# A hybrid encoder layer on one core: low parts and a rotary sum by adding DMAs, gate projections moved to the end of their stage

## The chip, the cores and the metric

The kernel runs on one core of a Trainium2 chip. TensorE (PE) multiplies matrices, VectorE (DVE), ScalarE (ACT) and GpSimd (POOL) work elementwise, and SyncE (SP) issues DMAs; each has a queue of its own that runs in order, and 16 DMA engines move the data. The metric is the device time of one execution in microseconds (us), the median of the runs of one kernel. Lower is better.

## The reference

One layer over 1024 tokens of width 1024, all in float32. Each sub-layer is wrapped in RMS norms, before and after, and its result is added to the residual stream.

```python
h = _rms_norm(x, g_mix_pre[l])
proj = h @ w_in[l]
aq, ak, av, dqkv, dgate, dalpha, dbeta = jnp.split(proj, IN_SPLITS, axis=-1)
aq = _rope(aq.reshape(b, s, ATTN_HEADS, ATTN_HEAD_DIM), positions)
ak = _rope(ak.reshape(b, s, ATTN_KV_HEADS, ATTN_HEAD_DIM), positions)
...
attn_o = _window_attention(aq, ak, av, attn_sink[l]).astype(x.dtype)
dn_o = _gated_deltanet(dqkv, dgate, dalpha, dbeta, ...).astype(x.dtype)
mix = jnp.concatenate([attn_o, dn_o], axis=-1) @ w_out[l]
x = x + _rms_norm(mix, g_mix_post[l])
c = _memory_cross_attention(_rms_norm(x, g_cross_pre[l]), _rms_norm(mem, g_mem[l]), ...)
x = x + _rms_norm(c, g_cross_post[l])
f = _swiglu(_rms_norm(x, g_ffn_pre[l]), w_gate_up[l], w_down[l])
x = x + _rms_norm(f, g_ffn_post[l])
```

The rotary embedding turns each head's two halves against each other: `x1*cos - x2*sin` and `x2*cos + x1*sin`. The attention is windowed (128 tokens to either side, 8 heads of 64, 2 key heads, a sink logit per head). The DeltaNet has 4 heads of 128, runs in both directions, and solves a triangular system in each block before a scan over blocks.

## The kernel before

**Split operands.** TensorE multiplies in a rounded format (fp32r). To keep float32 accuracy, an operand is held as a high part (the rounded value) and a low part (the value minus the high part), and each product is made of three matmuls: high by high, high by low, low by high. `split` (from L99) makes both parts: ScalarE rounds (L102), and VectorE, or GpSimd where the caller asks for it, subtracts (L103). `load_w` loads 512 KB of weights into a tile `wraw` (L125, on SP's queue) and splits it into `whi` and `wlo`. All three have two buffers, so a third load waits until the first raw tile has been read, and a third cast until the matmuls of the first are done. `load_w` runs at a raised priority, ahead of the work around it.

**Stages.** Stage 1 norms and turns the input, projects the DeltaNet's q, k and v (`proj`, matmuls at L261 into PSUM tiles `pg`, three buffers), convolves them on VectorE, and prepares the blocks; `base_inverse` inverts 32x32 blocks in a long chain of small VectorE operations (L534, L536), once for each pair of heads (`B0`, `B1`). Stage 2 has ten more projections, each of two halves of 512 tokens: A0 to A3 are the queries of the attention, A4 its keys, V its values, G0 to G3 the DeltaNet's gates. Beside them run the levels L0 to L3 (one for each DeltaNet head: SP fetches many small blocks of the inverse at L551, PE multiplies at L585 and L591, results are stored at L610), and the windows of the attention (`W` starts two of the 16 and ends the two before). Stage 3 scans the DeltaNet's blocks with the remaining windows and the memory's keys and values beside it. Then come the output projection, cross attention, its output projection, and the feed-forward layer.

**Attention tile.** `attn_proj` takes each half from PSUM, multiplies it by the sine into `sn` (tag "rot", two buffers, L729) and by the cosine into `rop` (two buffers, L730). Four DMAs on SP's queue bring the 32-row groups of `sn` to a tile `rot` in exchanged order (L734), and VectorE adds it (L735). The sum is split, and high and low parts are stored to memory (L739), where a window loads them again as `qs` (L625) or as keys (L679). `value_proj` copies its halves to `vT`, which uses the tag "rot" too (L746). `gate_proj` applies Silu and stores (L758, L759).

**Order.** The lists `ORDER_1` to `ORDER_3` give the program's order. A scheduler turns it into one queue per engine, by priority and by its own model of time, so the engines' queues interleave several items of a list; once built, a queue is fixed and runs in order.

**Mid norms.** `mid_gemm` (matmuls at L1016) makes an output projection for 512 tokens, normalises the result and adds the residual (L1030), then norms the new residual stream for the next sub-layer: ScalarE squares and sums (L1033), GpSimd takes the power (L162), ScalarE scales (L1036). It is called four times with four tiles of 128 tokens. PE then turns the scaled tiles.

**Constants.** `mhalf` and `phalf`, 16 columns each, hold -0.5 and 0.5 for GpSimd's power. They stand in the first pool on the left of the on-chip memory, ahead of the weight tiles.

Of the kernel before, what the change touches and what calls it, by code (L numbers as in the profile page):

```python
# [10 lines left out]
F32 = mybir.dt.float32  # L11
F32R = mybir.dt.float32r
I32 = mybir.dt.int32
AF = mybir.ActivationFunctionType
ALU = mybir.AluOpType
# [4 lines left out]
P = 128  # L20
# [4 lines left out]
HALF = 512  # L25
# [8 lines left out]


ORDER_1 = "D0 P0 D1 P1 D2 B0 P2 D3 P3 B1".split()
ORDER_2 = "L0 L1 G0 G1 A4 V A0 A1 L2 L3 W W W A2 A3 G2 G3 W".split()
ORDER_3 = ("M " + "s01 W K " * 5 + "s01 K " * 3 + "s01 V V").split()


# [35 lines left out]
def tile_hybrid_block(  # L76
# [6 lines left out]
    nc = tc.nc  # L83
    x, mem, out = x[0], mem[0], out[0]
    w_in, w_out, w_cq, w_ckv, w_co = w_in[0], w_out[0], w_cq[0], w_ckv[0], w_co[0]
    w_gate_up, w_down = w_gate_up[0], w_down[0]

    if dump is None:
        def dump(name, ap):
            pass  # L90


    def f32(ap):
        return ap.bitcast(F32)
# [4 lines left out]
    def split(hi, lo, src, scale=None, eng=None):  # L99

        if scale is None:
            nc.scalar.copy(hi, src)  # L102
            (eng or nc.vector).tensor_tensor(lo, src, f32(hi), ALU.subtract)  # L103
        else:
            nc.scalar.activation(hi, src, AF.Identity, scale=scale)
            nc.vector.scalar_tensor_tensor(lo, src, scale, f32(hi), ALU.mult, ALU.subtract)

    def pool(name, bufs, **kw):
        return tc.tile_pool(name=name, bufs=bufs, reuse_waits="tile", **kw)

    cst = ctx.enter_context(pool("cst", 1))
# [6 lines left out]
    def load_w(src, k, n, eng=None, after=None):  # L118

        with tc.high_priority(AHEAD):  # L120
            raw = wp.tile([P, k, n], F32, tag="wraw", name="wraw")
            with ExitStack() as order_:
                if after:
                    order_.enter_context(tc.issue_after(after.ins))
                nc.sync.dma_start(raw, src.rearrange("(k p) n -> p k n", p=P))  # L125
            hi = wp.tile([P, k, n], F32R, tag="whi", name="whi")
            lo = wp.tile([P, k, n], F32R, tag="wlo", name="wlo")
            split(hi, lo, raw, eng=eng)
        return hi, lo
# [2 lines left out]
    ident = cst.tile([P, P], F32, name="ident")  # L132
    mhalf = cst.tile([P, 16], F32, name="mhalf")
    nc.gpsimd.memset(mhalf, -0.5)
    phalf = cst.tile([P, 16], F32, name="phalf")
    nc.gpsimd.memset(phalf, 0.5)
    cols = cst.tile([P, P], F32, name="cols")
    p12 = ExitStack()
# [10 lines left out]
    trp = p1.enter_context(pool("trp", 2, side="right"))  # L149
# [61 lines left out]
    for hf in range(2):  # L211
        hi = hx.tile([P, KT, HALF], F32R, name=f"hhi{hf}")
        lo = hx.tile([P, KT, HALF], F32R, name=f"hlo{hf}")
        for j in range(4):
# [10 lines left out]
            for kq in range(2):  # L225
# [4 lines left out]
                o = slice(4 * kq, 4 * kq + 4), slice(j * P, (j + 1) * P)  # L230
# [25 lines left out]
    def gemm_b(whi, wlo, act, psums, nk=KT):  # L256

        for ah, p_ in zip(act, psums):
            for k in range(nk):
                for i, (w, a) in enumerate(((whi, 0), (whi, 1), (wlo, 0))):  # L260
                    nc.tensor.matmul(p_, w[:, k, :], ah[a][:, k, :], start=(k == 0 and i == 0),  # L261
                                     stop=(k == nk - 1 and i == 2))

    def proj(src_cols, eng=None):
        whi, wlo = load_w(src_cols, KT, P, eng)
        pp = [pg.tile([P, 512], F32, tag="pg", name="pg") for _ in range(2)]
        gemm_b(whi, wlo, hT, pp)
        return pp
# [42 lines left out]
    for hf in range(2):  # L311
        pp = pg.tile([P, 512], F32, tag="pg", name="pg")
# [390 lines left out]
    def issue(order, table):  # L703
        for o in order:
            table[o[0]](*(int(c) for c in o[1:]))
# [13 lines left out]
        nc.gpsimd.memset(t, 0.0)  # L719

    def attn_proj(ct):
        pp = proj(w_in[:, ct * P:(ct + 1) * P])
        dst = [t[ct * P:(ct + 1) * P, :] if ct < 4 else t for t in (d_q if ct < 4 else d_k)]
        for hf in range(2):
            sl = slice(hf * HALF, (hf + 1) * HALF)
            rop = trp.tile([P, HALF], F32, tag="rop", name="rop")
            sn = trp.tile([P, HALF], F32, tag="rot", name="sn")
            rot = trp.tile([P, HALF], F32, tag="rot2", name="rot2")
            nc.vector.tensor_tensor(sn, pp[hf], sinT[:, sl], ALU.mult)  # L729
            nc.vector.tensor_tensor(rop, pp[hf], cosT[:, sl], ALU.mult)  # L730

            for q in range(4):
                o = 32 * (q ^ 1)
                nc.sync.dma_start(rot[32 * q:32 * q + 32], sn[o:o + 32])  # L734
            nc.vector.tensor_tensor(rop, rop, rot, ALU.add)  # L735
            hl = [trp.tile([P, HALF], F32R, tag=t, name=t) for t in ("qhi", "qlo")]
            split(*hl, rop)
            for t, o in zip(hl, dst):
                nc.sync.dma_start(o[:, sl], f32(t))  # L739

    def value_proj():

        pp = proj(w_in[:, 640:768])
        for hf in range(2):
            vT = trp.tile([P, HALF], F32, tag="rot", name="vT")
            nc.scalar.copy(vT, pp[hf])  # L746
            pt = pw.tile([P, 512], F32, tag="pw", name="ptv")
            for j in range(4):
                nc.tensor.transpose(pt[:, j * P:(j + 1) * P], vT[:, j * P:(j + 1) * P], ident)
            pt = pt.rearrange("p (c g e) -> p c g e", c=4, g=2)  # L750
            split(*(vhl[:, 4 * hf:4 * hf + 4, :, i] for i in range(2)), pt)

    def gate_proj(h):

        pp = proj(w_in[:, 2304 + h * P:2304 + (h + 1) * P])
        for hf in range(2):
            gt = trp.tile([P, HALF], F32, tag="rop", name="gt")
            nc.scalar.activation(gt, pp[hf], AF.Silu)  # L758
            nc.sync.dma_start(d_gate[h * P:(h + 1) * P, hf * HALF:(hf + 1) * HALF], gt)  # L759

    issue(ORDER_2, {"A": attn_proj, "V": value_proj, "G": gate_proj, "L": levels, "W": next_windows})
    dump("d_q", d_q); dump("d_k", d_k); dump("d_gate", d_gate)
    p1.close()
# [201 lines left out]
    L0 = ExitStack()  # L965
# [33 lines left out]
    def mid_gemm(tz, act, w, gp, res, dst, hf, between=None):  # L999


        zs = [tz.tile([P, D], F32, tag="z", name="z", bufs=4) for _ in range(4)]
        sss = [tz.tile([P, 2], F32, tag="zss", name="zss", bufs=8) for _ in range(4)]
        for ch in range(2):
            cs = slice(ch * 512, (ch + 1) * 512)
            if ch and between:
                between()
            pp = [pg.tile([P, 512], F32, tag="pg", name="pmg") for _ in range(4)]
            for kp in range(4):
                whi, wlo = load_w(w[kp * 256:(kp + 1) * 256, cs], 2, 512)  # L1010
                for t in range(4):
                    tt = slice(t * P, (t + 1) * P)
                    for kk in range(2):
                        k = 2 * kp + kk
                        for i, (w_, a) in enumerate(((whi, 0), (whi, 1), (wlo, 0))):
                            nc.tensor.matmul(pp[t], act[a][:, k, tt], w_[:, kk, :], start=(k == 0 and i == 0),  # L1016
                                             stop=(k == KT - 1 and i == 2))
            for t in range(4):
                nc.scalar.activation(zs[t][:, cs], pp[t], AF.Square, accum_out=sss[t][:, ch:ch + 1])
                nc.vector.tensor_tensor(zs[t][:, cs], pp[t], gp[:, cs], ALU.mult)  # L1020
        xn = []
        for t in range(4):
            tok = slice(hf * HALF + t * P, hf * HALF + (t + 1) * P)
            z = zs[t]
            xr = tz.tile([P, D], F32, tag="xr", name="xr", bufs=XR)
            nc.sync.dma_start(xr, res[tok, :])
            rs = tz.tile([P, 1], F32, tag="prs", name="prs", bufs=4)
            nc.gpsimd.tensor_scalar(rs, sss[t][:, 1:2], sss[t][:, 0:1], D * EPS, ALU.add, ALU.add)
            nc.gpsimd.tensor_tensor(rs, rs, mhalf[:, 0:1], ALU.pow)
            nc.vector.scalar_tensor_tensor(z, z, rs, xr, ALU.mult, ALU.add)  # L1030
            nc.sync.dma_start(dst[tok, :], z)
            s2 = tz.tile([P, 1], F32, tag="ps2", name="ps2", bufs=4)
            nc.scalar.activation(xr, z, AF.Square, accum_out=s2)  # L1033
            r2 = tz.tile([P, 1], F32, tag="pr2", name="pr2", bufs=4)
            rstd_of(r2, s2, 1.0 / D, EPS)
            nc.scalar.activation(xr, z, AF.Identity, scale=r2)  # L1036
            xn.append(xr)
        return xn

# [4 lines left out]
    L1 = ExitStack()  # L1044
# [28 lines left out]
    L2 = ExitStack()  # L1073
# [63 lines left out]
    L3 = ExitStack()  # L1137
# [326 lines left out]
    for t in range(4):  # L1464
# [14 lines left out]
        xr = residual(r)  # L1479
# [40 lines left out]
```

## Time and profile before

| | |
|---|---|
| median of 3 runs | 1559.16 us (1558.93 to 1559.38) |
| profiled execution, its own time | 1562.86 us |
| its span | 1561.1 us |
| PE busy | 1504.1 us (96%) |
| VectorE busy | 1052.3 us (67%) |
| ScalarE busy | 726.5 us (47%) |
| GpSimd busy | 308.8 us (20%) |
| DMA, mean over the span | 158 GB/s |

In a timeline row stand the start and the length in us, the engine, the line, the operation, what it writes and reads, and in brackets the idle time of the engine before it with what ended that. A row of grouped instructions gives the least, the median and the greatest duration in ns, then the first and the last start in us. In a table by stretches the engines stand in the order PE, PE's weight loads, VectorE, ScalarE, GpSimd, each with its busy time and its number of instructions, then the granted PE clock (1.00 is full), the busy share of the DMA engines and their GB/s. A list of DMAs gives the KB of each and the median us from issue to landing.

### The profile page before, as it was taken

What the parts mean: (1) busy time and instruction counts of PE and PEld (TensorE: products, weight loads), DVE (VectorE), ACT (ScalarE), POOL (GpSimd) and SP (SyncE); (2) the same over time, 40 slices, a digit from 0 to 9 for tenths busy, and PEclk for the clock granted to TensorE, in tenths of its full rate; (3) what the DMA queues carried; (4) which work ended last, traced back from release to release, by engine and by line L of the source; (5) the groups of instructions that cost most, each with busy time, mean ns of one, the idle gap of its engine ahead of it and who ended that gap; (6) DMA issues with size and microseconds to landing.
All of it is one profiled execution on the core that took longest, in us unless ns stands there. A gap on an engine that the chain in (4) does not pass through costs nothing.

```text
span 1561.1 us, 20936 instructions
## 1 busy us (share of the span) xinstructions
PE 1504.1 (96%) x7451; PEld 1252.7 (80%) x7451; DVE 1052.3 (67%) x1742; ACT 726.5 (47%) x1388; POOL 308.8 (20%) x305
## 2 busy tenths in 40 slices
PE   6999999988999999999999999999999999999998
PEld 5888787877899777888888877888888888888786
DVE  6777888767998855434346377776867554696665
ACT  6665552346557765453336574322222222454532
POOL 2000110000004102153102221443433333000021
PEclk9999999999999999999999999999999999999999
DMA  6244446868987674354213254333433334753354
GB/s 208 70 130 121 130 146 159 219 176 273 336 268 251 199 268 149 116 169 147 68 54 135 97 190 139 115 125 119 157 119 109 101 102 138 286 195 102 108 174 164
DMA packets 267367, 247.17 MB, mean 158 GB/s; under 512 B 39016, under 2 KB 204797, under 8 KB 267261
## 3 DMA queue, kind: packets, MB, share of 16 engines
q1 hardware_dynamic: 267261, 245.82, 49.6%
q8 instruction: 59, 0.97, 0.2%
q14 instruction: 47, 0.39, 0.1%
HBM read 173.65 MB, written 69.50 MB: 156 GB/s over the span
## 4 chain that ended last, share of the span: by engine, by line
PE 78%; DVE 7%; DMA 6%; ACT 3%; issue 2%; SPq 2%; POOL 1%; DVEq 0%; POOLq 0%; ACTq 0%
PE pg L261 13%; PE pmg L1016 10%; PE pD L1191 8%; PE pE L1191 8%; PE pA L1191 6%; PE pcq L261 6%; PE pdX L1381 6%; PE pdA L1381 4%; PE pB L1191 4%; PE pdD L1381 2%; PE psc L785 2%; PE pcs L1097 1%; PE pco L1123 1%; DVE wlo L103 1%; PE pdX L1474 1%
## 5 line engine op out<-in xcount | busy, mean ns | idle before, releaser
L102 ACT CAST whi<-wraw 128x1024 fp32r<-128x1024 f32 x108 | 113.1, 1048 | 170.6 <-PE pg L261 38.4
L103 DVE TENSOR_TENSOR wlo<-wraw,whi 128x1024 fp32r<-128x1024 f32 x78 | 95.5, 1225 | 87.4 <-ACT whi L102 83.3
L261 PE MATMUL pg<-hhi,whi 128*128 128x512 f32 x352 | 142.1, 405 | 1.5 <-DVE rop L730 1.5
L261 PE MATMUL pg<-hhi,wlo 128*128 128x512 f32 x352 | 141.0, 401 | 0.0
L261 PE MATMUL pg<-hlo,whi 128*128 128x512 f32 x352 | 141.0, 401 | 0.0
L1016 PE MATMUL pmg<-whi,b 128*128 128x512 f32 x384 | 120.0, 399 | 2.6 <-ACT whi L102 2.2
L1191 PE MATMUL pA<-s,whi 128*128 128x512 f32 x352 | 111.4, 397 | 1.2 <-ACT m L1208 1.2
L103 POOL TENSOR_TENSOR wlo<-wraw,whi 128x1024 fp32r<-128x1024 f32 x30 | 73.9, 2464 | 147.0 <-ACT whi L102 138.8
L1016 PEld LDWEIGHTS pmg<-whi,b 128*128 128x128 f32 x384 | 72.2, 191 | 18.2 <-ACT whi L102 2.6
L261 PEld LDWEIGHTS pg<-hhi,whi 128*128 128x128 f32 x352 | 67.0, 191 | 16.7 <-DVE rop L730 2.0
L261 PEld LDWEIGHTS pg<-hlo,whi 128*128 128x128 f32 x352 | 67.0, 190 | 14.8
L1191 PEld LDWEIGHTS pA<-s,whi 128*128 128x128 f32 x352 | 65.2, 187 | 16.8 <-ACT m L1208 1.9
L261 PEld LDWEIGHTS pg<-hhi,wlo 128*128 128x128 f32 x352 | 66.7, 190 | 14.7
L1381 PE MATMUL pdX<-dhl,whi 128*128 128x512 f32 x264 | 76.1, 390 | 1.5 <-DVE zv L1436 0.8
L1016 PE MATMUL pmg<-wlo,b 128*128 128x512 f32 x192 | 71.5, 392 | 0.0
L1191 PE MATMUL pA<-s,wlo 128*128 128x512 f32 x176 | 69.7, 397 | 1.1 <-DVE wlo L103 1.1
L102 ACT CAST whi<-araw 128x1024 fp32r<-128x1024 f32 (+1 forms) x36 | 35.3, 982 | 71.3 <-PE pdX L1381 27.6
L1268 POOL TENSOR_TENSOR act<-act,up 128x512 f32<-128x512 f32 x33 | 50.1, 1519 | 91.1 <-DVE up L1267 54.3
L103 DVE TENSOR_TENSOR wlo<-araw,whi 128x1024 fp32r<-128x1024 f32 (+1 forms) x36 | 40.8, 1133 | 40.2 <-ACT whi L102 40.2
L286 DVE SCALAR_TENSOR_TENSOR acc<-cp,cols,acc 128x1024 f32<-128x1024 f32 x48 | 61.4, 1281 | 1.5 <-ACT acc L284 0.9
L1381 PEld LDWEIGHTS pdX<-dhl,whi 128*128 128x128 f32 x264 | 49.3, 188 | 12.8 <-issue 1.1
L1241 DVE TENSOR_TENSOR sr<-sr,wraw 128x512 f32<-128x512 f32 x22 | 38.1, 1732 | 29.1 <-POOL sr L1240 29.1
(408 smaller groups left out, 3971.9 us busy)
## 6 DMA issues: line engine op xcount, KB each, us to landing
wraw<-in_w_gate_up_dram SPq DMA_DIRECT2D x52, 512.0 KB, 3.9
kv<-d_kv SPq DMA_DIRECT2D x32, 512.0 KB, 6.7
wraw<-in_w_in_dram SPq DMA_DIRECT2D x22, 512.0 KB, 4.6
b<-in_w_down_dram SPq DMA_DIRECT2D x20, 512.0 KB, 6.8
araw<-d_as SPq DMA_DIRECT2D x20, 512.0 KB, 3.6
pz<-d_pz SPq DMA_DIRECT2D x32, 256.0 KB, 6.5
wraw<-in_w_ckv_dram SPq DMA_DIRECT2D x16, 512.0 KB, 7.1
wraw<-in_w_out_dram SPq DMA_DIRECT2D x16, 512.0 KB, 4.2
```

The source lines that it names most:

```text
L102: nc.scalar.copy(hi, src)
L103: (eng or nc.vector).tensor_tensor(lo, src, f32(hi), ALU.subtract)
L261: nc.tensor.matmul(p_, w[:, k, :], ah[a][:, k, :], start=(k == 0 and i == 0), stop=(k == nk - 1 and i == 2))
L286: nc.vector.scalar_tensor_tensor(acc, cp[:, t:t + S], taps[t], acc, ALU.mult, ALU.add)
L785: nc.tensor.matmul(out[:, d, h, :], lt[:, d, h, :], rt[:, d, h, :], start=True, stop=True)
L1016: nc.tensor.matmul(pp[t], act[a][:, k, tt], w_[:, kk, :], start=(k == 0 and i == 0), stop=(k == KT - 1 and i == 2))
L1097: nc.tensor.matmul(pp[:, t2_, :], q[a][:, ct, tt], kr_[b_][:, ct, :], start=(j == 0 and i == 0), stop=(j == 1 and i == 2))
L1123: nc.tensor.matmul(po, vr_[a][:, kt, cs], pts[kt][b_], start=(kt == 0 and i == 0), stop=(kt == 1 and i == 2))
L1191: nc.tensor.matmul(out_, w[a][:, k, :], xx[b_][:, k, :], start=(start and k == 0 and i == 0), stop=(k == HK - 1 and i == 2), skip_group_ch ...
L1241: nc.vector.tensor_tensor(s[1], s[0], a_[:, 0:HK], ALU.subtract)
L1268: nc.gpsimd.tensor_tensor(o_, o_, up, ALU.mult)
L1381: nc.tensor.matmul(banks[t], a[:, k - k0, tt], w, start=(first and k == 0 and i == 0), stop=(k == NB - 1 and i == 2), skip_group_check=not ...
```

## The change

Five edits:

1. The attention tile's rotary sum: the tile `rot`, the four copies on SP's queue and VectorE's addition go. Four DMAs on GpSimd's queue add the exchanged groups of `sn` into `rop` directly.
2. The low parts of the ten projections' weights: ScalarE writes the negated, rounded value into the low tile, and one DMA on GpSimd's queue, 512 KB, adds the raw weights to it. In `split` the value `nc.sync` for `eng` chooses this way.
3. `ORDER_2`: the two gate projections G0 and G1 move from ahead of A4 to behind A3, and V moves behind A1.
4. In `mid_gemm` VectorE does the last scaling in place of ScalarE.
5. The constant tile `phalf` is allocated with 32 columns, of which 16 are used.

```diff
-ORDER_2 = "L0 L1 G0 G1 A4 V A0 A1 L2 L3 W W W A2 A3 G2 G3 W".split()
+ORDER_2 = "L0 L1 A4 A0 A1 V L2 L3 W W W A2 A3 G0 G1 G2 G3 W".split()
...
         if scale is None:
             nc.scalar.copy(hi, src)
-            (eng or nc.vector).tensor_tensor(lo, src, f32(hi), ALU.subtract)
+            if eng is nc.sync:
+                nc.scalar.mul(lo, src, -1.0)
+                nc.gpsimd.dma_start(f32(lo), src, accum_op=ALU.add)
+            else:
+                (eng or nc.vector).tensor_tensor(lo, src, f32(hi), ALU.subtract)
...
-    phalf = cst.tile([P, 16], F32, name="phalf")
+    phalf = cst.tile([P, 32], F32, name="phalf")[:, 0:16]
...
     def attn_proj(ct):
-        pp = proj(w_in[:, ct * P:(ct + 1) * P])
+        pp = proj(w_in[:, ct * P:(ct + 1) * P], nc.sync)
...
-            rot = trp.tile([P, HALF], F32, tag="rot2", name="rot2")
             nc.vector.tensor_tensor(sn, pp[hf], sinT[:, sl], ALU.mult)
             nc.vector.tensor_tensor(rop, pp[hf], cosT[:, sl], ALU.mult)
 
             for q in range(4):
                 o = 32 * (q ^ 1)
-                nc.sync.dma_start(rot[32 * q:32 * q + 32], sn[o:o + 32])
-            nc.vector.tensor_tensor(rop, rop, rot, ALU.add)
+                nc.gpsimd.dma_start(rop[32 * q:32 * q + 32], sn[o:o + 32], accum_op=ALU.add)
...
-        pp = proj(w_in[:, 640:768])
+        pp = proj(w_in[:, 640:768], nc.sync)
...
-        pp = proj(w_in[:, 2304 + h * P:2304 + (h + 1) * P])
+        pp = proj(w_in[:, 2304 + h * P:2304 + (h + 1) * P], nc.sync)
...
-            nc.scalar.activation(xr, z, AF.Identity, scale=r2)
+            nc.vector.tensor_scalar(xr, z, r2, None, ALU.mult)
```

## The prediction

> **What bounds the kernel now.** I read the page first: one TensorE-bound program.
>
> ```profile
> span 1561.1 us, 20936 instructions
> PE 1504.1 (96%) x7451; PEld 1252.7 (80%) x7451; DVE 1052.3 (67%) x1742; ACT 726.5 (47%) x1388; POOL 308.8 (20%) x305
> PE 78%; DVE 7%; DMA 6%; ACT 3%; issue 2%; SPq 2%; POOL 1%; DVEq 0%; POOLq 0%; ACTq 0%
> ```
>
> PE is busy 1504 of 1561 us, so work taken off VectorE is worth nothing by itself. Only two things can be won: microseconds in which PE stands still, and those in which its clock is held down. Four of the five edits act in the second stage, where attention, value and gate projections run beside the DeltaNet levels (about 180 to 380 us). So the second view is the busy time by stretches there; its columns are PE, PE weight loads, DVE, ACT, POOL, clock, DMA share and GB/s.
>
> ```profile
> 180.00:220.00 40.00, 40.00 (x201) 33.19 (x200) 36.20 (x66) 24.50 (x42) 5.82 (x8) 1.00 0.46 135
> 220.00:260.00 40.00, 38.19 (x193) 31.61 (x191) 33.45 (x68) 7.55 (x12) 2.42 (x2) 1.00 0.62 161
> 260.00:300.00 40.00, 40.00 (x204) 34.15 (x205) 35.13 (x80) 12.36 (x30) 0.16 (x1) 0.91 0.74 203
> 300.00:340.00 40.00, 34.73 (x185) 29.12 (x184) 23.87 (x60) 12.69 (x34) 0.79 (x2) 0.96 0.75 192
> 340.00:380.00 40.00, 34.99 (x220) 30.21 (x220) 26.50 (x72) 28.99 (x68) 1.15 (x4) 0.99 0.73 215
> ```
>
> PE loses 1.8, 5.3 and 5.0 us in three of these five rows; VectorE is at 33 to 36 of 40 us in the first three; POOL does next to nothing; the DMA engines are three quarters full from 260 us. Third, the timeline of PE alone gives each stop with what ended it, and short stretches behind the stops give the clock.
>
> ```profile
> 259.96 1.12 PE L749 MATMUL ptv<-ident,vT 128*128 128x128 f32 x4 [1.81 <-ACT vT L746]
> 315.18 0.55 PE L633 MATMUL psw<-khi,qs 128*128 128x256 f32 x1 [3.67 <-DMA qs<-d_q]
> 335.28 0.50 PE L261 MATMUL pg<-hhi,whi 128*128 128x512 f32 x1 [1.52 <-DVE rop L730]
> 377.41 0.51 PE L664 MATMUL pow<-ph,vhl 128*128 128x512 f32 x1 [2.33 <-ACT ph L102]
> 379.39 0.77 PE L664 MATMUL pow<-pl,vhl 128*128 128x512 f32 x1 [1.48 <-DVE pl L103]
> ```
>
> ```profile
> 260.00:265.00 5.00, 5.00 (x18) 4.52 (x19) 4.68 (x15) 3.31 (x10) 0.00 (x0) 0.50 0.58 162
> 265.00:270.00 5.00, 5.00 (x26) 4.12 (x25) 4.84 (x12) 1.03 (x2) 0.00 (x0) 0.82 0.51 115
> 315.00:320.00 5.00, 4.82 (x22) 4.10 (x23) 2.33 (x7) 0.00 (x0) 0.00 (x0) 0.70 0.93 243
> 380.00:385.00 5.00, 5.00 (x29) 4.67 (x28) 3.63 (x9) 1.70 (x5) 1.19 (x2) 0.71 1.01 394
> ```
>
> Right behind three of the stops the granted clock is 0.50 to 0.82, so a stop costs more than its length: stop A (at 260) 1.81 + 5 x 0.50 + 5 x 0.18 = 5.2 us; stop B (at 315) 3.67 + 5 x 0.30 = 5.2; stop C (at 335) 1.5; stop D (at 377 to 379) 2.33 + 1.48 + 5 x 0.29 = 5.3. Together 17.2 us: the ceiling. Last the chain of waits for this stage (start, us, what): its stops hang on rotary copies and on what follows them.
>
> ```profile
> 257.20 2.02 DMA rot<-sn
> ...
> 289.92 2.64 DMA rot<-sn
> ...
> 300.28 5.74 DMA d_q<-qhi
> ...
> 310.00 4.94 DMA qs<-d_q
> ```
>
> **Part 1, rotary sum by adding DMAs.** Removed: 40 copies on SP's queue, ten additions on VectorE and one tile; added: 40 adding DMAs of the same 64 KB on POOL's queue. The rows are the copies' issue time (min/median/max ns), the addition, two moments of the first attention tile, and the time to landing.
>
> ```profile
> L734 SPq DMA_DIRECT2D rot<-sn x40: 507/588/1287, 255.3 to 343.9; - x40
> L735 DVE TENSOR_TENSOR rop<-rop,rot x10: 682/688/693, 259.3 to 347.9; 128x512 f32<-128x512 f32 x10
> 239.41 0.68 DVE L730 TENSOR_TENSOR rop<-pg,cosT 128x512 f32<-128x512 f32 x1
> 255.30 3.75 SPq L734 DMA_DIRECT2D rot<-sn x6
> rot<-sn SPq DMA_DIRECT2D x40, 64.0 KB, 2.6
> ```
>
> SP gets 40 x 0.588 = 23.5 us of issue time back, VectorE 10 x 0.688 = 6.9. The first tile's products are done at 240.1, and the copies leave SP only at 255.3: 15.2 us in a queue that first issues the stores and fetches of the levels. vT takes a buffer of the tag "rot", which those copies still read; that is stop A. On POOL there is no such line, so I count A as gone. The Trainium skill's page "DMA: Bandwidth & Descriptors" (section "Issuing engines are not separate DMA queues") speaks against this: issuing from another engine saves only issue time, "which is usually small relative to the DMA itself". By that rule part 1 would be worth about nothing and the sum would lose stop A's 5.2 us. The trace does not bear it out at that place, 15.2 us of queue standing against 2.6 us of transfer.
>
> What an adding DMA costs no row shows. From below: a copy, 0.59 to issue and 2.6 to land. From above: issue as the dearest small POOL operation (2.10 us for two, below) and twice the landing, since it reads two operands: 5.2. Four times 1.05 plus 5.2 is 9.4 us, less than the 15.2 + 3.75 it replaces, so either end hides.
>
> **Part 2, low parts by adding DMAs.** For the ten projections VectorE's subtraction goes; ScalarE writes the negated copy and a POOL DMA of 512 KB adds the raw weights.
>
> ```profile
> L102 ACT CAST whi<-wraw x10: 1028/1048/1054, 184.7 to 324.6; 128x1024 fp32r<-128x1024 f32 x10
> L103 DVE TENSOR_TENSOR wlo<-wraw,whi x10: 1215/1220/1225, 187.4 to 326.2; 128x1024 fp32r<-128x1024 f32 x10
> 238.56 1.05 ACT L102 CAST whi<-wraw 128x1024 fp32r<-128x1024 f32 x1 [9.11 <-PE pg L261]
> 249.76 1.05 ACT L102 CAST whi<-wraw 128x1024 fp32r<-128x1024 f32 x1 [10.15 <-PE pg L261]
> wraw<-in_w_in_dram SPq DMA_DIRECT2D x22, 512.0 KB, 4.6
> xr<-in_x_dram SPq DMA_DIRECT2D x8, 512.0 KB, 9.4
> 214.15 2.10 POOL L470 TENSOR_TENSOR rs<-rs,phalf 128x4 f32<-128x4 f32 x2 [24.06 <-DVE rs L469]
> 245.47 2.25 POOL L528 TENSOR_SCALAR_AFFINE_SELECT A<-A 128x1024 f32<-128x1024 f32 x1 [17.55 <-DVE A L527]
> ```
>
> VectorE saves 10 x 1.22 = 12.2 us, ScalarE gets 10 x 1.05 more at under half load. What counts is latency. A cast starts when PE releases a buffer pair, and its projection starts one projection later: that interval is the cover. Ten casts lie between 184.7 and 324.6, 15.5 us apart on average; the tight pair is 249.76 - 238.56 = 11.2. Today the weights are ready after 1.05 + 1.22 = 2.3 us. Afterwards: cast 1.05, negated copy 1.05, issue 0.59 to 1.05, landing from 4.6 (a plain load) to 9.4 (the slowest 512 KB row): 7.3 to 12.6. I take 1.05 and 7.0, the middle, since no row is nearer: 10.2, hidden by one microsecond. If the four rotary adds of a half (4 x 1.05 = 4.2) stand ahead on POOL it is 14.4, 3.2 more than a tight cover. In the new order five projections (A0, A1, V, A3, G0) come directly behind an attention tile; I take half of 3.2 for each: 8.0 us lost. Two queues can make it worse: on POOL an operation that waits holds all behind it (the affine select waited 17.55 us there), and on SP the raw load after next waits for the add, no longer for the subtraction, with the levels' fetches behind it. By the Trainium skill, the same page, section "Anatomy of one DMA — SWDGE (gpsimd) path", such a DMA takes 2.0 us plus its bytes at 436 GB/s; 3.2 us for 512 KB, or as my estimate from it 4.4 with two operands read. By that the 8.0 us would vanish and the gain would be 13.5; no run here shows an adding DMA yet.
>
> **Part 3, gate tiles last.** PE's work stays the same; the ten projections only change places. A4 comes two and A0 and A1 three places earlier, V stays fourth, and all four gates, which no other work of this stage waits for, stand behind A3. G3 is last but one in both orders, so the scan's first need of a gate comes no sooner. The queries of A0 and A1 are then stored before the first window asks, so stop B goes (5.2). Stop D is window work with nothing beside it after the last gate; with four gates there PE has filler, but the total is conserved: the stop goes only as far as the levels also end sooner. SP's 23.5 us and VectorE's 19.1 us speak for it; I count half, 2.6. Stop C (rop's buffers) I leave.
>
> **Part 4, mid norms; part 5, the constant tile.**
>
> ```profile
> L1036 ACT ACTIVATE xr<-z,pr x16: 1132/1152/1158, 617.4 to 917.7; 128x1024 f32<-128x1024 f32 x16
> L894 DVE TENSOR_SCALAR mt<-mt,mrs x2: 746/750/753, 379.9 to 381.3; 128x1024 f32<-128x1024 f32 x2
> 910.00:920.00 10.00, 8.95 (x42) 6.72 (x41) 2.11 (x3) 9.71 (x13) 1.63 (x5) 1.00 0.53 194
> ```
>
> Sixteen scalings of 1.15 us leave ScalarE; the same form on VectorE takes 0.75. Other matmuls cover them nearly everywhere; at 910 to 920, ScalarE is full and PE loses 1.05. I take 0.5 us gained, bounds 0 and 1. The wider constant tile shifts later left-hand tiles by 64 bytes. The ten casts alternate between two buffers within 1028 to 1054 ns, so I take nothing, 0.5 us either way.
>
> **Sum.** Gains 5.2 + 5.2 + 2.6 + 0.5 = 13.5, loss 8.0: 5.5 us less. The profiled execution took 1562.86 us (span 1561.1), 3.7 above the median of 1559.16; the difference is applied to the median: 1553.7.
>
> **Rivals.** (1) Slower: the low parts land late. Place: PE at the start of the ten projections. With a landing of 9.4 and rotary adds ahead the path is 16.8 us: 5.6 over the tight cover and 1.3 over the mean. 5 x 5.6 + 5 x 1.3 = 34.5, and 1.5 of lowered clock behind each of five stops: 42. Less 13.5 it is +28.5: 1587.7. It decides from a landing of 6.6 us if rotary adds always stand ahead (the path is then 7.35 plus the landing, and 5 x (7.35 + 6.55 - 11.2) = 13.5), and of 10.8 if never. For it: DMA shares near 0.75 and POOL's in-order queue. Against it: mostly wider covers. (2) The change wins nothing, because the levels' chain of fetches ends the stage as now and the stops only move: 1558.7 with hidden adds, 1566.7 with the 8.0 us. For it: DMA at 0.73 to 0.75 there, and adding DMAs bring more bytes. (3) Everything hides and all four stops go: 17.2 + 0.5, 1541.5; it belongs to the forecast's side.
>
> **How the numbers follow.** This kernel's measurement tells about 0.2%, 3.1 us, from no change. Forecast with (3) 0.52, rival (1) in any strength 0.30, rival (2) 0.18, half of it within 0.2% and half slower. That makes faster 0.52, same 0.09, slower 0.39. The forecast's own range is 1541 to 1556; the whole one, 1541 to 1584, leaves some 0.04 below (stops of the scan stage going too) and 0.12 above, the strongest of rival (1).
>
> **What would show it.** Right: no stop of PE ended by vT or qs near 260 and 315, full clock there, wlo's add landing within 8 us, the first scan matmul earlier. Wrong: PE stops at wlo before projections with a clock of 0.5 behind them, POOL issues over 1 us each, SP waiting for the add, or a stop as long as D before the scan.

## The result, and the profile after

The change makes the kernel slower: 1588.53 us in the median of six runs (1582.91 to 1592.78) against 1560.08 for the kernel before beside it (1558.93 to 1563.95), a ratio of 1.0172 with a 95% interval of 1.0146 to 1.0198. I had forecast 1553.7 us, and the result lies above the range, 1541 to 1584. The time stands near rival (1)'s 1587.7, but the runs below show that it is not that rival's mechanism: the nearness is chance.

The head of the profile's page after, then its busy time by stretches of 40 us (columns as in the prediction: PE, weight loads, VectorE, ScalarE, GpSimd, clock, DMA share, GB/s):

```profile
span 1591.1 us, 20985 instructions
PE 1520.3 (96%) x7451; PEld 1263.0 (79%) x7451; DVE 1056.3 (66%) x1738; ACT 718.0 (45%) x1382; POOL 352.1 (22%) x355
```

```profile
180.00:220.00 40.00, 40.00 (x198) 33.16 (x197) 36.01 (x66) 24.56 (x42) 11.43 (x15) 1.00 0.73 174
220.00:260.00 40.00, 37.09 (x175) 30.34 (x174) 27.86 (x50) 10.11 (x14) 18.75 (x24) 0.96 0.91 217
260.00:300.00 40.00, 35.75 (x178) 29.56 (x178) 30.33 (x85) 12.23 (x24) 17.02 (x21) 0.91 0.89 197
300.00:340.00 40.00, 31.17 (x158) 26.75 (x157) 12.42 (x29) 11.95 (x24) 1.94 (x3) 0.83 0.93 232
340.00:380.00 40.00, 39.75 (x239) 34.65 (x238) 23.69 (x67) 24.92 (x62) 0.39 (x2) 1.00 0.62 155
380.00:420.00 40.00, 31.80 (x169) 26.99 (x168) 27.75 (x77) 24.60 (x65) 2.26 (x7) 0.79 0.68 228
420.00:460.00 40.00, 33.92 (x242) 31.27 (x241) 31.30 (x85) 17.21 (x38) 0.40 (x2) 0.91 1.01 293
```

The last two stretches of the kernel before, which the prediction did not show:

```profile
380.00:420.00 40.00, 37.90 (x281) 35.10 (x280) 35.99 (x95) 24.61 (x58) 1.79 (x5) 0.96 1.03 344
420.00:460.00 40.00, 38.51 (x301) 36.41 (x301) 36.39 (x104) 18.40 (x45) 0.60 (x3) 1.00 0.95 320
```

Add the seven rows of each kernel. PE stands still 280 - 264.3 = 15.7 us before and 280 - 249.5 = 30.5 after: 14.8 more. The clock takes 40 x (0.09 + 0.04 + 0.01 + 0.04) = 7.2 us before and 40 x (0.04 + 0.09 + 0.17 + 0.21 + 0.09) = 24.0 after: 16.8 more. Together 31.6, against 30.0 us of longer span. So nearly all is lost between 220 and 460 us, about half as stops of PE and half as lowered clock, while VectorE's load falls and the DMA share rises from 0.46 to 0.75 up to 0.73 to 0.93 before 340 us. The largest stops of PE after, from its timeline:

```profile
242.38 0.50 PE L265 MATMUL pg<-hhi,wlo 128*128 128x512 f32 x1 [2.91 <-DMA wlo<-wraw]
268.73 1.05 PE L589 MATMUL ps<-m,L 128*128 128x32 f32 x8 [2.93 <-DMA m<-d_inv]
327.79 0.55 PE L637 MATMUL psw<-khi,qs 128*128 128x256 f32 x1 [8.60 <-DMA qs<-d_q]
406.39 0.98 PE L787 MATMUL psc<-kv,pz 128*128 128x128 f32 x3 [3.52 <-DMA pz<-d_pz]
455.39 0.53 PE L637 MATMUL psw<-klo,qs 128*128 128x256 f32 x1 [2.44 <-DMA klo<-d_k]
```

Only one of them waits for a low part. All five are ended by a DMA; stop B, at qs, has grown from 3.67 to 8.60 instead of going. What the adds cost, first the issue (ns min/median/max, first and last start), then from the page's list of DMAs the KB of each and the median us to landing:

```profile
L737 POOL DMA_DIRECT2D rop<-sn x40: 768/1384/2959, 204.6 to 296.5; - x40
```

```profile
wlo<-wraw POOLq DMA_DIRECT2D x10, 512.0 KB, 5.8
rop<-sn POOLq DMA_DIRECT2D x40, 64.0 KB, 5.2
```

The 512 KB add takes 5.8 us, less than the 7.0 that I had taken. The queue that stands longer is SP's. Its waits between 180 and 420 us (sum, times, longest), after:

```profile
SPq L129 <- DMA wlo<-wraw: 19.4, 5, 9.1
SPq L741 <- ACT qhi L102: 16.8, 4, 6.7
```

The row of before that answers to the first of these, where a raw load waits for VectorE's subtraction:

```profile
SPq L125 <- DVE wlo L103: 0.7, 1, 0.7
```

These two rows alone overstate the difference, since the view puts a wait down to whatever came last. All waits of SP's raw loads in this stretch, whatever they are put down to, add up to 11.5 us before and 19.7 after.

### The profile page after: what moved, and what is told of

It reads as the page before. It is cut to its first block, busy times and chain, and to the rows that moved or that the text cites. A ratio compares the mean times of both kernels' runs of the same rounds, so it can differ in the third digit from the quotient of the medians.

```text
span 1591.1 us, 20985 instructions
## 1 busy us (share of the span) xinstructions
PE 1520.3 (96%) x7451; PEld 1263.0 (79%) x7451; DVE 1056.3 (66%) x1738; ACT 718.0 (45%) x1382; POOL 352.1 (22%) x355
## 4 chain that ended last, share of the span: by engine, by line
PE 67%; DVE 5%; DMA 4%; ACT 2%; SPq 1%; issue 1%; POOL 0%; DVEq 0%; POOLq 0%; ACTq 0%
PE pmg L1018 11%; PE pD L1193 8%; PE pE L1193 7%; PE pA L1193 7%; PE pdX L1383 5%; PE pcq L265 5%; PE pdA L1383 4%; PE pB L1193 4%; PE psc L787 3%; PE pdD L1383 2%; PE pcs L1099 1%; PE pg L265 1%; PE pco L1125 1%; PE pdX L1476 1%; PE pck L918 1%
## 5 line engine op out<-in xcount | busy, mean ns | idle before, releaser
L107 DVE TENSOR_TENSOR wlo<-wraw,whi 128x1024 fp32r<-128x1024 f32 x68 | 83.3, 1226 | 79.6 <-ACT whi L102 76.9
L265 PEld LDWEIGHTS pg<-hlo,whi 128*128 128x128 f32 x352 | 68.1, 194 | 14.8
L1383 PEld LDWEIGHTS pdX<-dhl,whi 128*128 128x128 f32 x264 | 49.3, 188 | 12.7 <-ACT dhl L102 1.1
L1242 POOL TENSOR_TENSOR sr<-wraw 128x512 f32<-128x512 f32 x22 | 30.4, 1380 | 130.3 <-DMA wraw<-in_w_gate_up_dram 95.5
```

Source lines behind the costliest of these rows:

```text
L1242: nc.gpsimd.tensor_tensor(s[0], b_[:, 0:HK], b_[:, HK:], ALU.add)
L1383: nc.tensor.matmul(banks[t], a[:, k - k0, tt], w, start=(first and k == 0 and i == 0), stop=(k == NB - 1 and i == 2), skip_group_check=not ...
```

## The experiments

18 kernels ran, each beside the kernel before on the same chip. Edits are given against the kernel before or the changed kernel, as the expectation says. Two things limit what the differences say. The runs were made on several chips: a difference between two edited kernels shifts by up to some 2 us when each is first taken against the kernel before that ran beside it. And an edit also changes the order that the scheduler puts into the queues. Laid side by side, 196 of PE's 7451 matmuls stand at another place between the low parts alone and the same kernel without their adds, and 1061 between the rotary adds alone and the same with spare adds. Only the runs on the constant tile leave every queue as it was. Elsewhere a cost is that of the edit together with the orders that come with it.

### Which edit costs: one undone at a time

**The order undone.**

```diff
-ORDER_2 = "L0 L1 A4 A0 A1 V L2 L3 W W W A2 A3 G0 G1 G2 G3 W".split()
+ORDER_2 = "L0 L1 G0 G1 A4 V A0 A1 L2 L3 W W W A2 A3 G2 G3 W".split()
```

> The changed kernel with the order of before (gate tiles G0, G1 first, G2, G3 behind A3); all its adding DMAs, the mid norms on VectorE and the wider tile stay. Theory O (the order does the harm: seven tiles whose rotary work, stores and window loads share SP, VectorE and the DMA engines are packed into 204 to 296 us, beside the base inverse, and the gates no longer lie there): the 28 us go, 1552 to 1563 us, and the levels' V multiply comes back to about 230 us. Theory D (the adding DMAs do the harm, by their bytes and by waiting in POOL's in-order queue): it stays at 1580 to 1595, with a DMA share near 0.9 between 220 and 260 us.

Measured 1576.73 us, ratio 1.0100 (1.0070 to 1.0129): 12 us come back, 16 stay. Neither theory alone. The first base inverse ends early, at 222.8 us, and the levels' first matmul is still late, at 261.5 against 254.0 before.

**The order alone**, on the kernel before (the same line the other way).

> The kernel before with nothing but the new order of the tiles: copies and subtractions as before. Theory O: 1580 to 1592 us, most of the loss is here. Theory D, and the term of my sum for the gates last (5.2 + 2.6 us gained): 1549 to 1558. An interaction, where neither the order nor the adds alone do harm: within 1555 to 1563 here and in the run above.

Measured 1571.94 us, ratio 1.0072 (1.0047 to 1.0096): the order by itself loses 11 us, where I had counted 7.8 gained. VectorE's groups between 200 and 250 us show why (times, busy us, mean ns, then VectorE's idle time ahead of them), first before, then with the order alone:

```profile
L729 DVE TENSOR_TENSOR sn<-pg,sinT 128x512 f32<-128x512 f32 x2 | 1.4, 686 | 1.7 <-PE pg L261 1.7
L730 DVE TENSOR_TENSOR rop<-pg,cosT 128x512 f32<-128x512 f32 x2 | 1.4, 682 | 0.0
```

```profile
L735 DVE TENSOR_TENSOR rop<-rop,rot 128x512 f32<-128x512 f32 x6 | 4.1, 691 | 4.0 <-DMA rot<-sn 4.0
L103 DVE TENSOR_TENSOR qlo<-rop,qhi 128x512 fp32r<-128x512 f32 x6 | 4.1, 686 | 1.2 <-ACT qhi L102 1.2
L729 DVE TENSOR_TENSOR sn<-pg,sinT 128x512 f32<-128x512 f32 x6 | 4.1, 685 | 0.6 <-PE pg L261 0.6
L730 DVE TENSOR_TENSOR rop<-pg,cosT 128x512 f32<-128x512 f32 x6 | 4.1, 680 | 0.0
```

Before, 2.8 us of rotary work run beside the base inverse; now 16.4 us do, and VectorE stands 5.8 us (1.7 before) for their copies, casts and matmuls. A gate tile asks VectorE for nothing but its weights' subtraction. The inverse is a chain on VectorE, and its last step (the row's first and last start) moves from 230.2 to 250.2 us for the first pair of heads; before, then the order alone:

```profile
L538 DVE TENSOR_TENSOR V<-A,bB x2: 2031/2040/2049, 230.2 to 293.7; 128x1024 f32<-128x1024 f32 x2
```

```profile
L538 DVE TENSOR_TENSOR V<-A,bB x2: 1936/1992/2048, 250.2 to 308.4; 128x1024 f32<-128x1024 f32 x2
```

The levels can't start before it: their first matmul moves from 254.0 to 273.2, their last step from 372.7 to 385.5, and the scan from 382.9 to 393.5.

**The low parts undone** (in `split`, VectorE's subtraction again).

> The changed kernel with the ten low parts subtracted on VectorE again; rotary adds and the new order stay. Theory D in the form that the 512 KB adds are what delays the others: 1555 to 1566 us, and the rotary adds then land in under 4 us instead of 5.2 in the middle. Theory O: 1578 to 1592. My term for the low parts, 8.0 us lost, would give 1580.

Measured 1571.78 us, ratio 1.0064 (1.0044 to 1.0084): 16.7 us come back.

**The rotary sum undone** (copies on SP, addition on VectorE).

> The changed kernel with the rotary halves copied on SP's queue and added on VectorE again; low-part adds and the new order stay. Theory D in the form that the 40 rotary adds on POOL's queue delay: 1555 to 1566 us. Theory O: 1585 to 1600, since the order's seven tiles also get their copies back into SP's queue ahead of the levels' fetches (23.5 us of issue time).

Measured 1585.81 us, ratio 1.0153 (1.0134 to 1.0171): 2.7 us come back, within the scatter of these runs. In this order the forty small adds are not what costs.

### Each edit alone

**Low parts alone.**

```diff
-            (eng or nc.vector).tensor_tensor(lo, src, f32(hi), ALU.subtract)
+            nc.scalar.mul(lo, src, -1.0)
+            nc.gpsimd.dma_start(f32(lo), src, accum_op=ALU.add)
```

> The kernel before with nothing but the ten low parts made by ScalarE and an adding DMA. If the edits add up (the low parts cost 16.7 us between the changed kernel and the one with VectorE's subtraction, 13.9 between the order alone and the order with low parts): 1571 to 1578 us. If they only harm together with the new order: 1556 to 1564.

Measured 1585.41 us, ratio 1.0157 (1.0142 to 1.0172). More than either number: 24.6 us. In the old order it costs more than in the new one, so the edits do not add up. The kernel with the order undone, above, has these same low parts in the same order, with the rotary adds, the mid norms and the tile on top, and yet takes 1576.73, 8.7 us less. Beside the low parts' adds, then, it seems to help that forty copies leave SP's queue; no run takes that apart.

**Rotary sum alone.**

> The kernel before with nothing but the rotary sum by adding DMAs. My sum said that the stop at 260 us, ended by vT, goes: 1554 to 1557 us. If it is worth nothing, as the runs with and without it under the new order say (1571.8 with, 1571.9 without): 1558 to 1564.

Measured 1562.21 us, ratio 1.0013 (1.0002 to 1.0023): worth nothing or a little less. Stop A is gone, as forecast; what PE meets in its place, from its timeline:

```profile
256.67 0.83 PE L585 MATMUL ps<-m,L 128*128 128x32 f32 x6 [2.44 <-DMA m<-d_inv]
319.17 0.55 PE L633 MATMUL psw<-khi,qs 128*128 128x256 f32 x1 [6.87 <-DMA qs<-d_q]
```

PE comes to the levels' first matmul at 254.2 us, as before (254.0), but now it waits there: SP issues the fetches of `m` between 244.1 and 254.6 us, where before the last of them left at 251.8. Stop B grows from 3.67 to 6.87.

**Mid norms and tile together.**

> The kernel before with the mid norms' scaling on VectorE and the constant tile of 128 bytes, nothing else. My terms are 0.5 us gained and nothing: 1558 to 1562 us. A real gain of the mid norms would show as 2 us or more, and at 910 to 920 us PE would lose less than 1.05.

Measured 1565.03 us, ratio 1.0029 (1.0016 to 1.0042). Two edits that I had counted at 0.5 us gained cost 4; they are taken apart below.

### What the low parts' adds cost with

**A third raw buffer.** Each third of the ten loads goes to a tile of its own pool.

```diff
+            if eng is nc.sync and sum(extra) % 3 == 0:
+                raw = tl_.tile([P, k, n], F32, tag="wraw3", name="wraw", bufs=1)
```

> The changed kernel with a third buffer for the raw weights of the ten projections (each third load goes to a tile of its own). Theory S: what the low parts cost is SP's in-order queue, which stands 19.4 us in all waiting for an add to release the raw tile, with the levels' fetches and the stores behind it: that wait falls under 4 us and the time to 1570 to 1580. Theory B: it is the bytes and the lateness of the adds themselves: 1584 to 1592.

Measured 1590.89 us, ratio 1.0198 (1.0182 to 1.0213). The run does not decide: most of the wait that it was to take away is still there, 14.4 of 19.4 us.

```profile
SPq L135 <- DMA wlo<-wraw: 14.4, 3, 9.0
```

**Low parts by an operation of GpSimd.**

```diff
-                nc.scalar.mul(lo, src, -1.0)
-                nc.gpsimd.dma_start(f32(lo), src, accum_op=ALU.add)
+                nc.gpsimd.tensor_tensor(lo, src, f32(hi), ALU.subtract)
```

> The changed kernel with the ten low parts subtracted by an operation of GpSimd itself: no negated copy, no adding DMA, VectorE stays as free as in the changed kernel. If the adding DMAs do the harm (their bytes, their lateness, the raw tile that they hold): 1562 to 1576 us, as with VectorE's subtraction (1571.8) or better. If the harm is what a freer VectorE and a longer way to the weights do to the order of the queues: 1582 to 1595.

Measured 1579.84 us, ratio 1.0109 (1.0077 to 1.0140): between the two. 8.1 us above the subtraction on VectorE, 8.7 below the adding DMAs. So taking the ten subtractions off VectorE wins nothing in this form either. The run doesn't tell why: GpSimd takes 2.49 us for one in the middle, where VectorE took 1.22, they stand in GpSimd's queue with the rotary adds, and the orders differ.

**Spare adds of the raw weights**, beside VectorE's subtraction.

```diff
             split(hi, lo, raw, eng=eng)
+            if spare:
+                nc.gpsimd.dma_start(spare[0], raw, accum_op=ALU.add)
```

> The new order, the rotary adds, mid norms and the tile of the changed kernel, low parts on VectorE; beside each of the ten subtractions an adding DMA of the same 512 KB brings the raw weights into a spare tile that nobody reads. So the bytes, the issue on POOL and the hold on the raw tile are there, and no weight is late. Without these adds 1571.8 us, with real ones 1588.5. Lateness of the weights as the cause: 1570 to 1576. Bytes and holds as the cause: 1584 to 1592.

Measured 1604.03 us, ratio 1.0250 (1.0206 to 1.0294): 32 us for ten adds whose result nobody reads. But "no weight is late" did not come true. The raw tiles are held, ScalarE's casts wait 27.5 us in all for raw weights that land late, and the longest stop of PE hangs on one of these casts:

```profile
245.54 0.79 PE L265 MATMUL pg<-hhi,whi 128*128 128x512 f32 x1 [10.74 <-ACT whi L102]
```

So this run doesn't separate lateness from bytes and holds.

**Spare adds of resident data** (the source is a slice of `hT`, in pieces of 512 bytes).

> As the run before, but the ten spare adds read a part of the resident activations, so that no raw tile is held: only the bytes on the DMA engines and the issue on POOL's queue are left. Bytes as the cause: as the run before. The hold on the raw tile (SP's queue behind it) as the cause: 1570 to 1576 here, and 8 us or more above it in the run before.

Measured 1607.00 us, ratio 1.0283 (1.0241 to 1.0326). No raw tile is held, and it costs as much, so a loss of this size can come without the hold. These adds landed late themselves (7.3 to 12.7 us, median 9.1), with DMA shares of 1.02 to 1.07 from 220 to 340 us. They also hold GpSimd's queue: the second inverse's select there starts at 276.2 us, 5.9 after its input is ready, and the inverse's last step at 328.0 instead of 308.6 in the kernel without them.

**The negated copy without the add**, on the kernel before.

> The kernel before with the low parts' subtraction replaced by ScalarE's negated copy alone; the adding DMA is left out, so the low parts hold the wrong numbers. With the add this kernel took 1585.4 us (24.6 above before). The adding DMA as the cause: 1553 to 1565. ScalarE's added work and the changed order of the queues as the cause: 1580 to 1590.

Measured 1569.47 us, ratio 1.0044 (1.0027 to 1.0061). Of the 24.6 us of the low parts alone 15.9 come with the ten adding DMAs and the orders that belong to them, and 8.7 without, with ScalarE's copies and other queue orders. (Each against the kernel before beside it, 1560.86 and 1562.40, it is 17.5 and 7.1.) SP issues its loads, fetches and stores from 262 to 325 us in nearly the same order in both kernels, so its queue can be laid side by side: without the adds, then with them (start, length, the issues of one group).

```profile
265.77 1.80 SPq L554 DMA_DIRECT2D m<-d_inv  x4
271.54 2.04 SPq L554 DMA_DIRECT2D D<-d_inv  x4
290.76 5.75 SPq L554 DMA_DIRECT2D Z<-d_inv  x8
312.02 2.60 SPq L628 DMA_DIRECT2D qs<-d_q  x4
```

```profile
268.24 2.74 SPq L555 DMA_DIRECT2D m<-d_inv  x4
274.84 2.04 SPq L555 DMA_DIRECT2D D<-d_inv  x4
295.89 8.10 SPq L555 DMA_DIRECT2D Z<-d_inv  x8
320.81 2.67 SPq L629 DMA_DIRECT2D qs<-d_q  x4
```

SP falls behind by 2.5, 3.3, 5.1 and 8.8 us. No single wait is the loss. With the adds SP's 793 DMAs take 389.5 us to issue over the whole run, without them 379.2, while its raw loads wait about as long in both (19.4 and 17.5 us between 180 and 420 us). So it is the issues that take longer here, and the windows and levels that hang on that queue start later: the levels' last step at 394.1 instead of 377.3 us.

**Spare adds on the kernel before with the rotary adds** (source a contiguous part of `hT`).

> The kernel before with the rotary adds (1562.2 us by themselves) and ten spare adding DMAs of 512 KB, whose source is a contiguous part of the resident activations and whose target nobody reads; low parts on VectorE, old order. No weight is late and no raw tile is held. If the bytes on the DMA engines and POOL's queue are what the low parts' adds cost: 1572 to 1585 us. If it is the lateness or the hold on the raw tile: 1560 to 1567.

Measured 1583.10 us, ratio 1.0137 (1.0118 to 1.0155): 21 us above the rotary adds alone, with no raw tile held. SP's 753 DMAs take 374.9 us to issue over the whole run, 361.4 with the rotary adds alone. GpSimd's queue is loaded too: five of these adds wait on it for the one before, 19.2 us in all. But it isn't what holds the base inverse. The second inverse's select, on GpSimd, starts at 252.85 us, 0.1 after VectorE has made its input, and VectorE waited for a fetch (`bB<-d_beta`); with the rotary adds alone it starts at 246.85. The second inverse's last step starts at 307.0 instead of 295.4. What stays mixed is the bytes, GpSimd's queue for the rotary adds, and the orders.

### The order once more, and the two small edits

**A third gate ahead.**

```diff
-ORDER_2 = "L0 L1 G0 G1 A4 V A0 A1 L2 L3 W W W A2 A3 G2 G3 W".split()
+ORDER_2 = "L0 L1 G0 G1 G2 A4 V A0 A1 L2 L3 W W W A2 A3 G3 W".split()
```

> The kernel before with a third gate tile ahead: L0 L1 G0 G1 G2 A4 V A0 A1 L2 L3 W W W A2 A3 G3 W. The new order lost 11 us because it put six halves of rotary work, 16.4 us of VectorE between 200 and 250 us, beside the chain of the base inverse, whose end moved from 230.2 to 250.2 us. If VectorE beside the base inverse is what the order decides, one gate more does no harm there: the end of the chain stays at 222 to 231, and the time is 1554 to 1564 us. If any shift of the attention tiles to a later place costs (the windows wait for their queries): 1566 to 1575.

Measured 1569.86 us, ratio 1.0052 (1.0035 to 1.0069). The base inverse ends at 230.6 us, untouched, as the first theory wants, and yet 8 us are lost, as the second one said: the first window's matmuls move from 315.2 to 332.0, and between 340 and 380 us the clock is 0.79. So VectorE beside the base inverse isn't all that the order decides. Attention tiles cost at either side: earlier beside the base inverse, later by the windows.

**Mid norms alone.**

```diff
-            nc.scalar.activation(xr, z, AF.Identity, scale=r2)
+            nc.vector.tensor_scalar(xr, z, r2, None, ALU.mult)
```

> The kernel before with the mid norms' last scaling on VectorE and nothing else. Both small edits together took 1565.0 us, 4.2 above before, where I had counted 0.5 gained and nothing. If the scaling is what costs: 1563 to 1567 us. If the tile is: 1558 to 1562.

Measured 1559.86 us against 1561.63, ratio 0.9986 (0.9972 to 0.9999). It is the one edit that gains, 1.8 us with an interval from 0.2 to 4.4, and the only kernel of all that came out ahead of before, by less than the 0.2% that I hold to be telling. At 910 to 920 us, where PE had lost 1.05 us, it now loses nothing:

```profile
910.00:920.00 10.00, 10.00 (x48) 7.97 (x47) 8.29 (x12) 8.11 (x12) 2.85 (x5) 1.00 0.63 217
```

**The constant tile alone.**

```diff
-    phalf = cst.tile([P, 16], F32, name="phalf")
+    phalf = cst.tile([P, 32], F32, name="phalf")[:, 0:16]
```

> The kernel before with the constant tile of 128 bytes and nothing else: every tile left of it after that moves by 64 bytes. If the tile costs: 1563 to 1567 us. If the scaling does: 1558 to 1562.

Measured 1568.62 us, ratio 1.0044 (1.0028 to 1.0059). Every engine has the same instructions in the same order as before; only addresses differ. Up to 360 us this kernel is level with before or a little ahead. Then eight small fetches of the last level take longer to issue. Before, in the timeline (SP's fetches, and the matmuls that need them) and in two stretches:

```profile
359.27 5.06 SPq L551 DMA_DIRECT2D Z<-d_inv  x8
366.25 1.08 PE L585 MATMUL ps<-mov,L 128*128 128x64 f32 x8 [0.25 <-ACT Z L604]
```

```profile
365.00:370.00 5.00, 4.71 (x35) 4.09 (x34) 4.19 (x14) 3.07 (x9) 0.00 (x0) 1.00 0.37 111
370.00:375.00 5.00, 4.10 (x28) 3.25 (x27) 3.47 (x9) 3.92 (x8) 0.20 (x1) 1.00 0.65 193
```

With the wider tile:

```profile
359.69 6.22 SPq L551 DMA_DIRECT2D Z<-d_inv  x8
367.29 0.41 PE L585 MATMUL ps<-mov,L 128*128 128x64 f32 x2 [1.56 <-ACT Z L605]
```

```profile
365.00:370.00 5.00, 3.42 (x20) 2.71 (x19) 3.30 (x12) 2.47 (x8) 0.00 (x0) 0.84 0.42 120
370.00:375.00 5.00, 5.00 (x23) 4.90 (x22) 1.79 (x6) 1.33 (x3) 0.00 (x0) 0.50 0.11 31
```

A stop of 0.25 us has become one of 1.56. Behind it the clock is 0.50 for the next 5 us, so the level's last matmuls take nearly twice as long (eight at L591 1.80 us instead of 1.00), and the scan starts at 388.0 instead of 382.9: behind 1.3 us more of standing still come 5.1. Over the whole span the mean granted clock is 0.9899 before and 0.9855 with the wider tile. If PE worked all that time, that is 15.7 and 22.7 us, and the difference is the tile's 7.0.

**The changed kernel without the tile.**

> The changed kernel with the constant tile of 16 columns again, everything else of the change stays; every engine's order of instructions is the changed kernel's. By itself the tile cost 7.0 us, on an order in which it made one fetch of a level 1.3 us late. If that cost is a constant one: 1579 to 1584 us. If it is a matter of which stop a shifted fetch happens to meet, it need not come back here: 1585 to 1592.

Measured 1578.02 us, ratio 1.0114 (1.0100 to 1.0128): the tile's cost stands in the changed kernel too, 10.5 us, again with equal queues. More than a third of the whole loss is an edit that computes nothing. Here the scan starts at 400.9 instead of 406.4, and the memory's values at 550.8 instead of 561.3.

**A shift of 128 bytes** (48 columns, on the kernel before).

> The kernel before with a constant tile of 48 columns: the same edit as the tile alone, but the tiles behind it move by 128 bytes in place of 64; every engine's order of instructions is that of before. If the cost hangs on how tiles lie within 128 bytes: 1559 to 1563 us. If any shift of them costs: 1565 to 1570.

Measured 1565.59 us, ratio 1.0020 (1.0009 to 1.0030): 3.8 us, at the lower end of the second range. It is less than for 64 bytes and more than nothing; why a shift moves the transfers at all stays open.

## Why the prediction was wrong, by its steps

**The bound** was read rightly: time is won or lost in PE's stops and clock, and a stop costs more than its length. The place was drawn too narrowly: the loss reaches to 460 us, behind the 380 where the prediction's table ends, and three edits act there directly, not four, since the mid norms run from 617 us on.

**Part 3 is the step that failed by sign.** I counted 7.8 us gained for the gates last (all of stop B, half of D), and the order alone costs 11. I named VectorE's 33 to 36 of 40 us in the table and then cost the move on PE and on the windows only. "All four gates, which no other work of this stage waits for" is true, and it is why they were the right work beside the base inverse: they ask almost nothing of VectorE, on which that chain runs. In place of the 7.8 us gained, the chain's last step came 20 us later, the levels' first matmul 19 and the scan 11. The A0 and A1 queries are stored earlier, from 232 us on in the changed kernel; their loads still leave SP only at 322.9, behind the stores and fetches of the second base inverse, so stop B grew.

**Part 2 failed by mechanism.** I priced the low parts by their lateness, 8.0 us. The landing was 5.8 us, better than I took, and of PE's waits for `wlo` only one was long, 2.91 us. The adds cost some 16 us in the old order, where no long stop of PE waits for `wlo`. "On SP the raw load after next waits for the add ... with the levels' fetches behind it" named the right queue, and I gave it no term in the sum; but it isn't the wait that grew there (19.4 us with the adds, 17.5 without), it is the time that SP takes to issue, 10.3 us more. Why issues take longer beside the adds no run takes apart. In the new order even that isn't the path: the sum is 364.9 us in the changed kernel and 362.1 with the low parts undone, and how its 16.7 us come about stays open. By the rule of the Trainium skill ("DMA: Bandwidth & Descriptors", section "Anatomy of one DMA — SWDGE (gpsimd) path") this loss should have vanished; the measured landing, 5.8 us, is above both 3.2 and my estimate of 4.4, and PE stood only 3.1 us for it in the changed kernel.

**Part 5 failed by size**: nothing, 0.5 either way, measured 7.0 alone and 10.5 in the change. I looked at the casts' durations, which indeed do not move, and not at transfers.

**Part 1**: stop A went, as said, and the 5.2 us did not come with it; alone the edit is at 1562.21 against 1560.86. That is what the other rule of that page of the Trainium skill (section "Issuing engines are not separate DMA queues") says it is worth, and the runs agree with it in the sum: 1.4 us the wrong way, where I had put 5.2 the right way. PE's stop moved to the levels' fetch and to stop B. My bounds for the add, landing 2.6 to 5.2 and issue 0.59 to 1.05, were low: 5.2 in the middle, 8.5 at most, and 1.38 in the middle.

**Part 4** was right in place: 0.5 counted, 1.8 measured, with an interval that holds both; the scaling's median on VectorE was 0.754 us, as taken.

**The rivals.** Rival (1) has nearly the number, by luck, and not the mechanism. Rival (2), that the levels' chain of fetches ends the stage and adding DMAs bring more bytes, had the place; its price, at most 8 us, was the miss. One by one the edits cost 11 + 24.6 + 1.4 - 1.8 + 7.0 = 42 us, and 28.4 together. That they spend the same slack is a reading that no run tests.

## What to carry to other kernels

Before work is moved next to a long chain, ask for each engine of that chain what the moved work wants from it; PE's filler must not be VectorE's load. A DMA that replaces an operation is priced by the in-order queues and the transfers it runs beside, and not by its own landing alone: here adds that PE hardly waited for cost some 16 us, while SP's fetches slid by up to 8.8. Test edits one by one, the ones that compute nothing included.

## What the runs showed of the hardware that I had not expected

- Behind a stop of PE one microsecond longer can come a loss of five: after 0.25 us at 366 the clock was 1.00 over the next 5 us, after 1.56 it was 0.50, in two kernels with the same instructions in the same order. It isn't the length alone, since before's stop of 1.52 us at 335 was followed by a clock of 1.00 up to 355. In all these traces a stretch at 0.50 between two at 1.00 lasts 3.4 us or a multiple of it (up to 23.9), so with PE busy the loss comes in steps of 1.7 us. The Trainium skill ("TensorE: Matmul & The Clock Gate", section "HAM oscillation — how this bites in real kernels") has as its rule that PE should have no idle gap above some 3.4 us; here half of that was followed by half clock (1.56 us, and 1.81 at stop A), and the measurement decides.
- 64 bytes of on-chip memory ahead of the weight tiles cost 7.0 us with every queue unchanged, 128 bytes cost 3.8, and in the changed kernel 64 bytes cost 10.5.
- An adding DMA of 64 KB that crosses partitions took 1.38 us to issue and 5.2 to land in the changed kernel, where the copy before took 0.59 and 2.6. One of 512 KB took 5.8 there and 4.9 with the low parts alone, and 9.1 in the run whose source lay in pieces of 512 bytes.
